# Decoder trunk with a state-space branch: buffers, load times and memory type of the state-space matrices and of the split u are changed

## The chip, the core and the metric

The kernel runs on one core of a Trainium2 chip. Its engines have instruction queues of their own and work beside each other: TensorE (PE, with PEld for the loading of its weights), VectorE (DVE), ScalarE (ACT), GpSimd (POOL) and SyncE (SP). The last two are used here mostly to issue transfers, which 16 DMA engines carry out. The metric is the device time of one execution in microseconds; less is better.

## The reference, cut to what matters

Two layers work on one sequence of 256 tokens of width 2048, all in float32. A layer has a mixer and an MLP:

```python
def hybrid_mixer(x, ...):
    q, k, v, u = parts of x @ w_in          # u: 1024 columns, 64 groups of 16
    gate_a, gate_s = sigmoid(x @ ...), sigmoid(x @ ...)
    attn = diff_attention(rope(q), rope(k), v, ...)
    ssm  = s5_ssm(u, ...)                   # a complex state of 64 per group
    merged = gate_a * (attn @ w_attn_up) + gate_s * (ssm @ w_ssm_up)
    return merged @ w_out

x = layer_norm(ALPHA * x + hybrid_mixer(x))
x = layer_norm(ALPHA * x + (relu(x @ w_mlp_up) ** 2) @ w_mlp_down)   # 2048 -> 8192 -> 2048

def s5_ssm(u, ...):                         # per group, per token
    bu = u @ b                              # 16 channels -> 64 complex states
    s  = running sum of bu with decay a     # the scan
    y  = Re(c s) + d u
    g  = gelu(y);  return g * sigmoid(g @ w_glu)
```

What matters below: `b` is made of four blocks per layer (here `bT`, 256 KB each, 1 MB per layer), u is the product of x with the first columns that a layer computes, and `bu` joins the two.

## The kernel before

**Products.** Every float32 product is done as three float32r products. An operand is split into a high part, which is the value rounded to float32r, and a low part, which is what is left: `split` copies the high part on ACT (L142) and subtracts it on DVE (L144). Then high x high, high x low and low x high are summed in PSUM. The weights pass through the core once: `load` fetches a chunk of 512 KB on SP's queue (L343) into one of four raw buffers (tile `w`), and splits it into `whi` and `wlo`, of which there are three each. One chunk is loaded ahead of the one in use (AHEAD = 1), and the scheduler puts the load as early as the buffers allow. A chunk feeds 24 matmuls of 256 columns in `gemm_feat` (L528 to L530), whose result has features on the partitions, or 12 of 512 columns in `gemm_tok` (L453, L454, L457).

**Background work.** The state-space branch, the attention and other small things are Python generators that `Background` runs beside the weight products: after each chunk `bg.pump(rate)` gives credit, and a generator runs until its `yield` costs have used it up. The rate is 2.0 a chunk in the mixer of layer 0, 1.8 in that of layer 1 and 0.3 in the MLP. So the order in which instructions are written comes from these costs; the scheduler then arranges each engine's queue. Each engine takes its queue in order.

**Buffers.** Scratch tiles of 128 x 512 come from two small sets: `t_bg` (tag `ss`, four buffers) for background work and `t_fg` (tag `at`, three) for evacuations of the products. Big tiles come from 17 slots of 8 KB per partition, and a slot is free again when the last reader of its tile is done.

**The state-space matrices.** `b_gen` handles the four blocks of a layer one after the other: it loads the block (L545, on POOL's queue) into an `ss` tile, splits it into two more (L142, L144), and writes high, low and high to a scratch tensor in DRAM, `bsplit` (L551, three writes of 256 KB). For layer 0 this runs in the first stage, behind the rotary tables and the parameters of the state space: `prep = [rope_gen(), ssm_param_gen(), b_gen(0)]`. For layer 1 it runs in the MLP of layer 0, as the first thing that is added to the background behind `down(0)`, ahead of tables (`emem`, `cmem`) for the same branch. There the load is held (`hold`) behind the products in front of it.

**u.** `u_evac` copies a finished part of u from PSUM to the slot `uT` (L891), splits it into two `at` tiles and writes three pieces to DRAM, `usplit` (L894, 256 KB each). A layer has four such parts, so 12 writes, in each layer's first products (layer 1: behind the first half of v).

**Where they meet.** `ssm_gen` loads, for each of 16 steps, a piece of `bsplit` (tile `bs`, L623) and a piece of `usplit` (tile `us`, L625) on POOL's queue, one buffer each, and multiplies them on PE (L646, four matmuls into `bu`). PE's queue holds these between the weight products.

Of the kernel before, what the change touches and what calls it, by code (L numbers as in the profile page):

```python
# [11 lines left out]
F32 = mybir.dt.float32  # L12
F32R = mybir.dt.float32r
# [7 lines left out]
P = 128  # L21
# [45 lines left out]


class Background:
    """Work that runs beside the weight products, a few instructions at a time."""  # L70

    def __init__(self):
        self.gens = []
# [31 lines left out]
def trunk(ctx: ExitStack, tc: tile.TileContext, A, out):  # L105
# [13 lines left out]
    def nm(s):  # L119
        uid[0] += 1  # L120
        return f"{s}_{uid[0]}"
# [4 lines left out]
    def t_bg(shape):  # L126
        return tmp.tile(shape, F32, tag="ss", name=nm("ss"), bufs=SS_BUFS)
# [20 lines left out]
    after = mybir.DependencyInfo(mybir.DependencyClass.NoSync, mybir.DependencyReason.DATA)  # L148

    class Chain:  # L150
        """Keeps instructions of one engine in the order given."""

        def __init__(self):
            self.last = None
# [268 lines left out]
    behind = mybir.DependencyInfo(mybir.DependencyClass.Sync, mybir.DependencyReason.DATA)  # L423

    def spread(dst, src):
        """Moves a [128, 2048] block in four parts, each behind the next products."""
        for c in range(4):
            cs = slice(c * W, c * W + W)
            drip.append((dst[:, cs], src[:, cs]))
# [1 line left out]
    recent = [None]  # L431

    def hold(i):
        """Keeps work that could run at any time behind the products in front of it."""
        if recent[0] is not None:
            tc.add_manual_dep(i.ins, recent[0].name, behind, reason="not before")
        return i
# [101 lines left out]
    bsplit, cmem, emem = {}, {}, {}  # L539

    def b_gen(l):
        bsplit[l] = dram.tile([4, 4, 3, 32, 2, 256], F32R, tag=f"bsplit{l}", name=f"bsplit{l}")
        for g in range(4):
            raw, hi, lo = (t_bg([P, 2, 256]) for _ in range(3))
            i = GP.dma_start(raw, A["bT"][l, g])  # L545
            if l > 0:
                hold(i)
            hi, lo = hi.bitcast(F32R), lo.bitcast(F32R)
            split(hi, lo, raw)
            for m, t in enumerate((hi, lo, hi)):  # L550
                GP.dma_start(bsplit[l][g, :, m], t)  # L551
            yield 0.6

    def e_steps(l, g, im, re, hold=lambda i: i):
# [49 lines left out]
    def ssm_gen(l, st):  # L604
# [13 lines left out]
        def operands(i):  # L618
            if i == 16:
                return None  # L620
            g, h, kk = i // 4, i // 2 % 2, i % 2
            bs = tmp.tile([96, 2, 2, P], F32R, tag="bs", name=nm("bs"), bufs=1)
            GP.dma_start(bs.rearrange("p q c s -> p q (c s)"), bsplit[l][g, 2 * kk:2 * kk + 2, :, :, h].rearrange("q m r s -> (m r) q s"))  # L623
            us = tmp.tile([96, 2, 256], F32, tag="us", name=nm("us"), bufs=1)
            GP.dma_start(us, st["split"][2 * kk:2 * kk + 2, :, :, 2 * g + h].rearrange("q m r t -> (m r) q t"))  # L625
            return bs, us
# [3 lines left out]
        for g in range(4):  # L630
# [10 lines left out]
            for k in range(4):  # L641
                bs, us = nxt
                bu = psa.tile([P, 2, 2, NCH, L], F32, tag="bu", name=nm("bu"), bufs=1)
                for q in range(2):
                    for ri in range(2):
                        PE.matmul(bu[:, q, ri].rearrange("p a b -> p (a b)"), bs[:, q, ri, :], us[:, q, :].bitcast(F32R), start=True, stop=True)  # L646
                nxt = operands(4 * g + k + 1)
                yield 0.3
                er = e_re[:, g, 2 * k:2 * k + 2, None, :].broadcast_to([P, 2, NCH, L])
                ei = e_im[:, g, 2 * k:2 * k + 2, None, :].broadcast_to([P, 2, NCH, L])  # L650
                wr, wi = (w[ri][:, :, 2 * k:2 * k + 2, :].rearrange("p c q t -> p q c t") for ri in range(2))
                ta, tb = t_bg([P, 2, NCH, L]), t_bg([P, 2, NCH, L])
                V.tensor_tensor(wr, bu[:, :, 0], er, op=ALU.mult)
                V.tensor_tensor(ta, bu[:, :, 1], ei, op=ALU.mult)
                V.tensor_tensor(wi, bu[:, :, 1], er, op=ALU.mult)
                yield 1.8
                V.tensor_tensor(tb, bu[:, :, 0], ei, op=ALU.mult)
                V.tensor_tensor(wr, wr, ta, op=ALU.add)
                V.tensor_tensor(wi, wi, tb, op=ALU.subtract)
                yield 1.8  # L660
# [205 lines left out]

        return evac

    prep = [rope_gen(), ssm_param_gen(), b_gen(0)]
    first = True  # L870

    for l in range(DEPTH):
# [9 lines left out]
        sgen = early()  # L882
        first = False
        uT = slot([P, 8, 256], name="uT")
        st["split"] = dram.tile([4, 3, 32, 8, 256], F32, tag=f"usplit{l}", name=f"usplit{l}")

        def u_evac(b, ps):
            ct = 4 * n + 2 * b
            u = uT[:, ct:ct + 2, :]
            hi, lo = t_fg([P, 2, 256]), t_fg([P, 2, 256])  # L890
            SC.activation(u, ps, AF.Copy)  # L891
            split(hi.bitcast(F32R), lo.bitcast(F32R), u)
            for m, t in enumerate((hi, hi, lo)):
                GP.dma_start(st["split"][:, m, :, ct:ct + 2], t)  # L894
# [192 lines left out]
def _layout(i):  # L1087
# [23 lines left out]
    for ri, s in enumerate(("re", "im")):  # L1111
        b = f["ssm_b_" + s].reshape(DEPTH, 8, 4, 2, 64, 16)
        c = f["ssm_c_" + s].reshape(DEPTH, 8, 4, 2, 16, 64)
        for g in range(2):
            bT[:, :, g, :, :, ri, g, :] = b[:, :, :, g].transpose(0, 2, 4, 1, 3)
            cT[:, g, :, ri, :, :, g, :] = c[:, :, :, g].transpose(0, 4, 1, 2, 3)
    o["bT"] = bT.reshape(DEPTH, P, 4, 2, 2 * P).transpose(0, 2, 1, 3, 4)
    o["cT"] = cT.reshape(DEPTH, P, 2, 4, 8, 32).transpose(0, 3, 1, 2, 4, 5)
    return {k: np.ascontiguousarray(v) for k, v in o.items()}

# [16 lines left out]
```

## Time and profile before

| | |
|---|---|
| runs, us | 2781.41, 2788.29, 2786.13 |
| median, us | 2786.13 |
| profiled execution, us | 2782.7 (its span; the page gives no time around the span) |
| PE busy | 2709.6 us, 97% |
| DVE busy | 1865.6 us, 67% |
| ACT busy | 1271.2 us, 46% |
| POOL busy | 146.4 us, 5% |
| DMA, mean over the span | 193 GB/s |

Shares of busy time are of the whole span. The slices of the span show where it is not alike. Each digit is a fortieth of the span, about 70 us, in tenths:

```profile
PE   7899999999999889999998999999999999999997
DMA  8756555674655666655748565556746565555673
```

The first slices, those at the 14th to 15th place (about 900 to 1040 us) and at the 22nd (about 1460 to 1530 us) are where PE is below nine tenths, apart from the last slice. In the first layer the u product starts the span; the 14th and 15th slice lie in the MLP of layer 0, and the 22nd in the u product of layer 1.

### The profile page before, as it was taken

The numbers are of one execution on the slowest core, as the hardware profiler recorded it, in microseconds if no ns is written. First come the engines' busy times: TensorE is split into PE (matmuls) and PEld (weight loads), VectorE is DVE, ScalarE is ACT, GpSimd is POOL, SyncE is SP. The second block draws the span as 40 slices with busy tenths as digits, with TensorE's granted clock in tenths as the row PEclk, the third lists the DMA queues.
The fourth block names the chain that finished last, engine by engine and source line by source line (L and its number), as shares of the span: only waits on it lengthen the run. The fifth ranks groups of instructions, "written<-read, shape, count | busy, mean of one in ns | idle before, by whom it ended". The sixth has DMA issues, their size and how long they took to land. (4 is left out here: it accounts for less than half of the span.)

```text
span 2782.7 us, 45210 instructions
## 1 busy us (share of the span) xinstructions
PE 2709.6 (97%) x18304; PEld 2487.0 (89%) x18304; DVE 1865.6 (67%) x2555; ACT 1271.2 (46%) x1635; POOL 146.4 (5%) x274
## 2 busy tenths in 40 slices
PE   7899999999999889999998999999999999999997
PEld 7889999988998888998788999999789989989876
DVE  5798999666655456655655998987766555545555
ACT  4554554544444344443443645544444444434442
POOL 2100000000000100000012000001000000000000
PEclk9999999999999999999999999999999999999999
DMA  8756555674655666655748565556746565555673
GB/s 269 202 182 198 173 168 167 212 238 131 207 182 189 186 196 205 222 189 194 237 154 238 176 191 175 168 174 222 255 131 203 183 194 186 188 191 184 193 230 127
DMA packets 169440, 536.27 MB, mean 193 GB/s; under 512 B 32112, under 2 KB 38288, under 8 KB 169232
## 3 DMA queue, kind: packets, MB, share of 16 engines
q1 hardware_dynamic: 133344, 482.40, 53.5%
q0 software_dynamic: 35888, 50.99, 6.9%
q8 instruction: 143, 2.34, 0.3%
q14 instruction: 65, 0.53, 0.1%
HBM read 513.32 MB, written 19.92 MB: 192 GB/s over the span
## 5 line engine op out<-in xcount | busy, mean ns | idle before, releaser
L144 DVE TENSOR_TENSOR wlo<-w,whi 128x1024 fp32r<-128x1024 f32 (+1 forms) x884 | 1076.8, 1220 | 696.1 <-ACT whi L142 694.6
L142 ACT ACTIVATE whi<-w 128x1024 fp32r<-128x1024 f32 (+1 forms) x884 | 934.0, 1058 | 1177.6 <-PE g L529 627.7
L528 PE MATMUL g<-xT,whi 128*128 128x256 f32 x3712 | 1058.0, 286 | 20.8 <-ACT whi L142 20.8
L530 PE MATMUL g<-xT,wlo 128*128 128x256 f32 x3712 | 1050.1, 287 | 23.3 <-DVE wlo L144 23.3
L529 PE MATMUL g<-xT,whi 128*128 128x256 f32 x3712 | 1056.9, 286 | 0.0
L528 PEld LDWEIGHTS g<-xT,whi 128*128 128x128 f32 x3712 | 722.0, 195 | 24.1 <-ACT whi L142 22.4
L530 PEld LDWEIGHTS g<-xT,wlo 128*128 128x128 f32 x3712 | 715.7, 195 | 28.6 <-DVE wlo L144 27.3
L529 PEld LDWEIGHTS g<-xT,whi 128*128 128x128 f32 x3712 | 721.9, 195 | 1.6 <-issue 1.2
L454 PE MATMUL g<-wlo,hT 128*128 128x512 f32 x972 | 379.1, 390 | 4.8 <-DVE wlo L144 4.8
L453 PE MATMUL g<-whi,hT 128*128 128x512 f32 x972 | 378.8, 390 | 0.8 <-ACT whi L142 0.8
L457 PE MATMUL g<-whi,hT 128*128 128x512 f32 x972 | 299.3, 389 | 0.0
L454 PEld LDWEIGHTS g<-wlo,hT 128*128 128x128 f32 x972 | 182.5, 188 | 44.9 <-DVE wlo L144 7.4
L453 PEld LDWEIGHTS g<-whi,hT 128*128 128x128 f32 x972 | 182.5, 188 | 40.1 <-ACT whi L142 2.8
L457 PEld LDWEIGHTS g<-whi,hT 128*128 128x128 f32 x972 | 182.5, 188 | 37.9
L454 PE MATMUL g<-wlo,merged 128*128 128x512 f32 x216 | 85.4, 395 | 2.6 <-DVE wlo L144 2.4
L453 PE MATMUL g<-whi,merged 128*128 128x512 f32 x216 | 84.3, 390 | 0.8 <-ACT whi L142 0.8
L671 DVE TENSOR_TENSOR_SCAN sw<-ss,sw 128x512 f32<-128x512 f32 x64 | 75.8, 1211 | 0.0
L529 PE MATMUL g<-sgl,whi 128*128 128x256 f32 x256 | 72.3, 283 | 0.0
L528 PE MATMUL g<-sgl,whi 128*128 128x256 f32 x256 | 72.0, 283 | 0.0
L530 PE MATMUL g<-sgl,wlo 128*128 128x256 f32 x256 | 72.0, 283 | 0.0
L529 PE MATMUL g<-ahl,whi 128*128 128x256 f32 x256 | 71.8, 284 | 0.0
L528 PE MATMUL g<-ahl,whi 128*128 128x256 f32 x256 | 71.4, 284 | 0.0
(284 smaller groups left out, 2774.3 us busy)
## 6 DMA issues: line engine op xcount, KB each, us to landing
w<-in_w_mlp_up_dram SPq DMA_DIRECT2D x256, 512.0 KB, 3.5
w<-in_w_mlp_down_dram SPq DMA_DIRECT2D x256, 512.0 KB, 3.6
w<-in_w_in_dram SPq DMA_DIRECT2D x255, 512.0 KB, 3.9
w<-in_w_out_dram SPq DMA_DIRECT2D x64, 512.0 KB, 4.4
w<-in_w_attn_up_dram SPq DMA_DIRECT2D x32, 512.0 KB, 3.7
w<-in_w_ssm_up_dram SPq DMA_DIRECT2D x32, 512.0 KB, 4.5
w<-in_w_glu_dram SPq DMA_DIRECT2D x16, 512.0 KB, 3.8
lnb<-in_ln_dram POOLq DMA_DIRECT2D x32, 256.0 KB, 4.6
```

Of the source, the lines that this page charges most:

```text
L142: SC.activation(hi, src, AF.Copy, scale=scale)
L144: V.tensor_tensor(lo, src, hi.bitcast(F32), op=ALU.subtract)
L453: mm(PE.matmul(ps[tt], act(kt)[:, 0, ts], hi[:, k, :], start=kt == 0, stop=False))
L454: mm(PE.matmul(ps[tt], act(kt)[:, 0, ts], lo[:, k, :], start=False, stop=False))
L457: mm(PE.matmul(ps[tt], act(kt)[:, 1, ts], hi[:, k, :], start=False, stop=kt == nkt - 1))
L528: m(PE.matmul(o, wh, ah, start=first and b % 2 == 0, stop=False))
L529: m(PE.matmul(o, wh, al, start=False, stop=False))
L530: m(PE.matmul(o, wl, ah, start=False, stop=last and b % 2 == 1))
L671: V.tensor_tensor_scan(wv, rg, wv, 0.0, ALU.mult, ALU.add)
```

## The change

`b_gen` gets buffers of its own from the slots: one for the four raw blocks (`braw`) and two for the split ones (`bhl`). The four loads are issued first, each held behind the products in front of it and 0.3 of credit apart. Then comes other work: in layer 0 the parameters of the state space, which stood ahead of `b_gen` before, and for layer 1 a pause of 2.0 of credit. Then the four blocks are split and written, 0.6 apart, and each high part is held behind the products in front of it. u's halves go to two slots (`uhl`) instead of `at` tiles. `bsplit` and the tile `bs` are plain float32, and the matmul reads `bs` as float32r. The host's layout of `bT` puts the four blocks of a partition side by side. The other edits empty comments.

```diff
     def b_gen(l):
-        bsplit[l] = dram.tile([4, 4, 3, 32, 2, 256], F32R, tag=f"bsplit{l}", name=f"bsplit{l}")
+        raw = slot([P, 4, 2, 256], name="braw")
         for g in range(4):
-            raw, hi, lo = (t_bg([P, 2, 256]) for _ in range(3))
-            i = GP.dma_start(raw, A["bT"][l, g])
-            if l > 0:
-                hold(i)
-            hi, lo = hi.bitcast(F32R), lo.bitcast(F32R)
-            split(hi, lo, raw)
+            hold(GP.dma_start(raw[:, g], A["bT"][l][:, g]))
+            yield 0.3
+        if l == 0:
+            yield from ssm_param_gen()
+        else:
+            yield 2.0
+        bsplit[l] = dram.tile([4, 4, 3, 32, 2, 256], F32, tag=f"bsplit{l}", name=f"bsplit{l}")
+        hi, lo = (slot([P, 4, 2, 256], name="bhl") for _ in range(2))
+        for g in range(4):
+            h = SC.activation(hi[:, g].bitcast(F32R), raw[:, g], AF.Copy)
+            hold(h)
+            V.tensor_tensor(lo[:, g].bitcast(F32R), raw[:, g], hi[:, g], op=ALU.subtract)
             for m, t in enumerate((hi, lo, hi)):
-                GP.dma_start(bsplit[l][g, :, m], t)
+                GP.dma_start(bsplit[l][g, :, m], t[:, g])
             yield 0.6
...
-            bs = tmp.tile([96, 2, 2, P], F32R, tag="bs", name=nm("bs"), bufs=1)
+            bs = tmp.tile([96, 2, 2, P], F32, tag="bs", name=nm("bs"), bufs=1)
...
-                        PE.matmul(bu[:, q, ri].rearrange("p a b -> p (a b)"), bs[:, q, ri, :], us[:, q, :].bitcast(F32R), start=True, stop=True)
+                        PE.matmul(bu[:, q, ri].rearrange("p a b -> p (a b)"), bs[:, q, ri, :].bitcast(F32R), us[:, q, :].bitcast(F32R), start=True, stop=True)
...
-    prep = [rope_gen(), ssm_param_gen(), b_gen(0)]
+    prep = [rope_gen(), b_gen(0)]
...
         uT = slot([P, 8, 256], name="uT")
+        uhl = [slot([P, 8, 256], name="uhl") for _ in range(2)]
...
-            hi, lo = t_fg([P, 2, 256]), t_fg([P, 2, 256])
+            hi, lo = (t[:, ct:ct + 2, :] for t in uhl)
...
-    o["bT"] = bT.reshape(DEPTH, P, 4, 2, 2 * P).transpose(0, 2, 1, 3, 4)
+    o["bT"] = bT.reshape(DEPTH, P, 4, 2, 2 * P)
```

The numbers of loads, splits, writes and matmuls are what they were. What moves is the order on ACT and POOL. On PE the weight products keep their order, and the first four `bu` matmuls of layer 0 stand behind 460 of them; before, one stood behind 412 and three behind 432.

ACT in the first stage, before, from its first state-space split on (`whi` is the high part of a weight chunk, `ss` of a state-space block, `uT` a part of u copied out of PSUM, `at` its high part):

```order
L142 ACTIVATE ss_501<-ss_500 128x512
L142 ACTIVATE whi_424<-w_422 128x1024
L142 ACTIVATE whi_471<-w_469 128x1024
L142 ACTIVATE ss_510<-ss_509 128x512
L142 ACTIVATE whi_547<-w_545 128x1024
L891 ACTIVATE uT_167<-g_170 128x512
L142 ACTIVATE whi_596<-w_594 128x1024
L142 ACTIVATE at_527<-uT_167 128x512
L891 ACTIVATE uT_167<-g_171 128x512
L287 ACTIVATE scr_315<-scr_315 128x64
L289 ACTIVATE scr_315<-scr_315 128x64
L142 ACTIVATE at_535<-uT_167 128x512
```

And after (`bhl` is the high part of a state-space block, `uhl` that of a part of u, L287 and L289 belong to the parameters):

```order
L142 ACTIVATE whi_530<-w_528 128x1024
L287 ACTIVATE scr_322<-scr_322 128x64
L289 ACTIVATE scr_322<-scr_322 128x64
L555 ACTIVATE bhl_507<-braw_317 128x512
L142 ACTIVATE whi_575<-w_573 128x1024
L900 ACTIVATE uT_167<-g_172 128x512
L900 ACTIVATE uT_167<-g_173 128x512
L142 ACTIVATE uhl_168<-uT_167 128x512
L555 ACTIVATE bhl_507<-braw_317 128x512
L142 ACTIVATE uhl_168<-uT_167 128x512
L555 ACTIVATE bhl_507<-braw_317 128x512 x2
L142 ACTIVATE whi_618<-w_616 128x1024
```

The first state-space split moves from behind the seventh weight split (`whi_377`) to behind the tenth (`whi_530`); the four now stand within two chunks, and all their loads are issued ahead of them.

POOL in the first stage, before, up to the first load of `us`; three writes of `bsplit` stand ahead of these rows (`ss` are blocks and their halves, `at` halves of u, `bs` and `us` the loads for `bu`):

```order
L551 DMA bsplit_499<-ss_510 4x32x512 x2
L545 DMA ss_518<-in_bT_dram 128x512
L623 DMA bs_896<-bsplit_499 96x2x256
L551 DMA bsplit_499<-ss_511 4x32x512
L894 DMA usplit_168<-at_527 4x32x512 x2
L894 DMA usplit_168<-at_535 4x32x512 x2
L894 DMA usplit_168<-at_528 4x32x512
L551 DMA bsplit_499<-ss_519 4x32x512 x2
L551 DMA bsplit_499<-ss_520 4x32x512
L545 DMA ss_575<-in_bT_dram 128x512
L894 DMA usplit_168<-at_536 4x32x512
L625 DMA us_898<-usplit_168 96x2x256
```

And after; two writes of `bsplit` stand ahead of these rows:

```order
L559 DMA bsplit_506<-bhl_508 4x32x512
L903 DMA usplit_170<-uhl_168 4x32x512 x2
L559 DMA bsplit_506<-bhl_507 4x32x512 x2
L903 DMA usplit_170<-uhl_168 4x32x512 x2
L903 DMA usplit_170<-uhl_169 4x32x512
L559 DMA bsplit_506<-bhl_507 4x32x512 x4
L559 DMA bsplit_506<-bhl_508 4x32x512
L903 DMA usplit_170<-uhl_169 4x32x512
L559 DMA bsplit_506<-bhl_508 4x32x512
L631 DMA bs_881<-bsplit_506 96x2x256
L559 DMA bsplit_506<-bhl_508 4x32x512
L633 DMA us_883<-usplit_170 96x2x256
```

No load of a block stands between the writes now, and 18 writes stand ahead of the first `us` where it was 15.

POOL in the MLP of layer 0, before, from the first block's load on:

```order
L545 DMA ss_9907<-in_bT_dram 128x512
L551 DMA bsplit_9906<-ss_9908 4x32x512 x2
L545 DMA ss_9976<-in_bT_dram 128x512
L551 DMA bsplit_9906<-ss_9909 4x32x512
L551 DMA bsplit_9906<-ss_9977 4x32x512 x2
L551 DMA bsplit_9906<-ss_9978 4x32x512
L545 DMA ss_10045<-in_bT_dram 128x512
L623 DMA bs_14694<-bsplit_9906 96x2x256
L551 DMA bsplit_9906<-ss_10046 4x32x512 x2
L545 DMA ss_10114<-in_bT_dram 128x512
L551 DMA bsplit_9906<-ss_10047 4x32x512
L551 DMA bsplit_9906<-ss_10115 4x32x512 x2
```

And after:

```order
L546 DMA braw_9891<-in_bT_dram 128x512 x4
L559 DMA bsplit_10211<-bhl_10212 4x32x512 x2
L559 DMA bsplit_10211<-bhl_10213 4x32x512
L559 DMA bsplit_10211<-bhl_10212 4x32x512 x2
L631 DMA bs_14664<-bsplit_10211 96x2x256
L559 DMA bsplit_10211<-bhl_10213 4x32x512
L559 DMA bsplit_10211<-bhl_10212 4x32x512 x2
L559 DMA bsplit_10211<-bhl_10213 4x32x512
L559 DMA bsplit_10211<-bhl_10212 4x32x512 x2
```

Each load stood behind a write of an earlier block, and the split needs the load; now the four loads stand ahead of all writes.

## Rows read from the trace of the kernel before

**Rows 1.** Page of the profile: span, and busy time of each engine.

```profile
span 2782.7 us, 45210 instructions
...
PE 2709.6 (97%) x18304; PEld 2487.0 (89%) x18304; DVE 1865.6 (67%) x2555; ACT 1271.2 (46%) x1635; POOL 146.4 (5%) x274
```

**Rows 2.** Stretches: us; busy of PE, PEld, DVE, ACT, POOL; clock; DMA share; GB/s.

```profile
25.00:100.00 75.00, 61.30 (x440) 59.88 (x441) 43.33 (x112) 27.89 (x37) 21.15 (x31) 0.89 0.84 237
720.00:740.00 20.00, 20.00 (x169) 20.00 (x168) 11.07 (x11) 9.48 (x12) 0.00 (x0) 1.00 0.57 189
940.00:1000.00 60.00, 44.75 (x284) 43.14 (x283) 22.34 (x25) 18.24 (x24) 10.07 (x16) 0.81 0.64 173
1455.00:1510.00 55.00, 46.85 (x365) 46.10 (x364) 26.54 (x31) 20.13 (x23) 16.79 (x26) 0.94 0.90 267
```

**Rows 3.** Waits of ACT, 25 to 100: waiting <- waited for, us, times, longest.

```profile
ACT ss L142 <- DMA ss<-in_bT_dram: 20.4, 3, 7.9
ACT whi L142 <- DMA w<-in_w_in_dram: 17.2, 5, 7.1
```

**Rows 4.** Waits, 900 to 1000 us.

```profile
ACT ss L142 <- DMA ss<-in_bT_dram: 28.4, 3, 13.1
...
DVE ss L560 <- DMA bsplit<-ss: 7.2, 1, 7.2
```

**Rows 5.** Timeline of ACT, MLP of layer 0: start, length; idle before in brackets.

```profile
968.17 0.63 ACT L142 ACTIVATE ss<-ss 128x512 fp32r<-128x512 f32 x1 [13.06 <-DMA ss<-in_bT_dram]
```

**Rows 6.** Timeline of POOL, same stretch.

```profile
952.56 2.03 POOL L551 DMA_DIRECT2D bsplit<-ss  x3 [11.71 <-ACT ss L142]
954.59 0.60 POOL L545 DMA_DIRECT2D ss<-in_bT_dram  x1
```

**Rows 7.** Waits, 1455 to 1510 us.

```profile
ACT whi L142 <- DMA w<-in_w_in_dram: 21.0, 5, 8.8
...
DVE at L144 <- DMA usplit<-at: 7.7, 1, 7.7
```

**Rows 8.** DMA issues, 935 to 1000: count, KB each, median us to landing.

```profile
w<-in_w_mlp_up_dram SPq DMA_DIRECT2D x14, 512.0 KB, 9.4
bsplit<-ss POOLq DMA_DIRECT2D x12, 256.0 KB, 10.1
ss<-in_bT_dram POOLq DMA_DIRECT2D x3, 256.0 KB, 12.0
emem<-ss POOLq DMA_DIRECT2D x2, 256.0 KB, 4.9
bs<-bsplit POOLq DMA_DIRECT2D x1, 192.0 KB, 14.1
```

**Rows 9.** Page: costliest groups; count, busy us, mean ns, idle before.

```profile
L144 DVE TENSOR_TENSOR wlo<-w,whi 128x1024 fp32r<-128x1024 f32 (+1 forms) x884 | 1076.8, 1220 | 696.1 <-ACT whi L142 694.6
```

**Rows 10.** Timeline of ACT, first stage.

```profile
30.99 1.06 ACT L142 ACTIVATE whi<-w 128x1024 fp32r<-128x1024 f32 x1 [1.44 <-PE g L529]
```

**Rows 11.** Timeline of POOL, first stage.

```profile
28.44 1.51 POOL L551 DMA_DIRECT2D bsplit<-ss  x2 [6.88 <-ACT ss L142]
...
65.66 0.67 POOL L625 DMA_DIRECT2D us<-usplit  x1 [6.52 <-DMA usplit<-at]
```

**Rows 12.** Timeline of PE, first stage.

```profile
75.52 0.28 PE L646 MATMUL bu<-us,bs 96*128 96x256 f32 x1
```

**Rows 13.** DMA issues, 25 to 100.

```profile
w<-in_w_in_dram SPq DMA_DIRECT2D x19, 512.0 KB, 9.6
bsplit<-ss POOLq DMA_DIRECT2D x12, 256.0 KB, 10.6
usplit<-at POOLq DMA_DIRECT2D x12, 256.0 KB, 15.0
...
us<-usplit POOLq DMA_DIRECT2D x2, 192.0 KB, 11.3
```

**Rows 14.** Page: DMA issues over the whole span.

```profile
w<-in_w_in_dram SPq DMA_DIRECT2D x255, 512.0 KB, 3.9
```

## The prediction

> **What bounds the kernel now.** The first view is the page: TensorE (PE) is busy 97% of the span [rows 1], so nothing off PE is worth anything unless PE waits for it there. The next question is where PE waits. The view by stretches shows three places. In a calm stretch PE does 169 matmuls in 20 us, 8.45 a microsecond, at a DMA share of 0.57 and 189 GB/s [rows 2]; that is the yardstick. In the first stage (25 to 100 us) it does 440 in 75 us. At its pace these need 52.1 us, so 22.9 us are lost. In the MLP of layer 0 (940 to 1000) it does 284 in 60 us: 33.6 us of work, 26.4 lost. In the u product of layer 1 (1455 to 1510) it does 365 in 55 us: 43.2 us of work, 11.8 lost. Part of the loss is idle time and part a lower granted clock behind it (0.89, 0.81 and 0.94 over these stretches, so partly at the lower of its two levels, 1.2 GHz, against 1.00 or 2.4 GHz in the calm one); counting matmuls takes both. Together 61.1 us, the most that this change can give back.
>
> The view of waits says why. PE waits for weight parts (`whi`, `wlo`), and their makers stand still. In the first stage ACT spends 20.4 us in three waits for the load of the state-space matrix, ahead of weight splits that could run [rows 3]. In the MLP of layer 0 it spends 28.4 us so, also in three waits, and DVE 7.2 us until a write of `bsplit` has landed, because the next scratch tile shares its buffers [rows 4]. ACT and DVE take their instructions in order, so one early split holds up every weight behind it. The chain of one of them: the load stands on POOL's queue behind three writes of the group before, it lands late, and ACT idles 13.06 us [rows 5, 6]. In layer 1 it is DVE, 7.7 us until a write of `usplit` frees an `at` tile [rows 7]. A second kind of wait stands beside these: ACT for the weights' own loads, 17.2 us in the first stage and 21.0 in layer 1 [rows 3, 7]. This kind the change does not touch.
>
> **The change part by part.** Splits and writes keep their count (4 ACT and 4 DVE splits, 12 writes per layer for the matrices; the same for u), so no engine gains work. The order of ACT and POOL tells what moves.
>
> *Layer 0's MLP.* The four loads are now issued a chunk or so apart, then 2.0 units of background credit pass, then come the splits 0.6 apart. At 0.3 credits a chunk these are (1.2 + 2.0 + 2.4) / 0.3 = 18.7 chunks of 24 matmuls, 2.84 us each by the yardstick: 53 us. The first split stands over 20 us behind its load, and a load took 12.0 us there in the median [rows 8]. So the 28.4 us of ACT waits go, and with own buffers the 7.2 us of DVE go. What is late next is the transfers: the stretch moved 0.64 x 60 = 38.4 us of all 16 DMA engines; its weights are 33.6 x 0.57 = 19.2 us of that, so the 18 other transfers listed there cost 19.2 us, about 1.07 us each [rows 2, 8]. Spread over 53 us they add 0.36 to 0.57: a share of 0.93, which fits, barely. The splits' hold behind a product costs ACT nothing while it comes with the release of a weight buffer that ACT awaits anyway; if that cover is gone it is 1.06 + 1.22 us a split [rows 9, 10], below 10 in all. Between 15 and 26 us returned; I take 24, near the full loss, since the share fits.
>
> *First stage.* All four loads go out in one piece and their splits come behind the first chunks, after the parameters. The 20.4 us of ACT waits go. But here the DMA engines are nearly full: 0.84 x 75 = 63 us of work [rows 2]. The same bytes cannot take less than 63 us (12 us returned), and at the 0.90 that the stretch in layer 1 sustained they take 70 (5 returned). The second half of the u writes may land later, where the share is low: six writes at 1.07 us, up to 6 more. On the other side POOL's queue now has 18 writes ahead of the first load of `us`, and before 15. Before, those from 28.44 on and the loads between took until 65.66 us: 37.2 us for 15 writes, 2.5 us a write [rows 11]. The first split now stands behind ACT's tenth weight split; the ninth started at 30.99 [rows 10], and a chunk later the writes can begin, at about 36 us. At the old pace the load would then be issued at 81 and, with the 11.3 us that such a load took [rows 13], land at 92.3. PE's first `bu` product, with all weight products queued behind it, stands behind 460 weight products in the new order and behind 412 in the old, where it started at 75.52 [rows 12]. At this stretch's 5.87 products a microsecond the 48 more are 8.2 us, so it would be due at 83.7, and the stage would be 9 us slower. But much of that 2.5 us was POOL waiting for ACT's late splits, and this goes. Between -9 and 18 returned; I take 11, nearer the share's bound than the old pace.
>
> *u product of layer 1.* Own tiles for both halves end DVE's 7.7 us. The transfers need 0.90 x 55 = 49.5 us [rows 2], so by them 5.5 us can go at most if all stay in the stretch, and all 11.8 if the last writes slip out of it. ACT's 21.0 us of waits for weights [rows 7] are the transfers' own and stay. Between 0 and 11; I take 5, the share's bound.
>
> *Plain float32 memory.* The matmul reads the same bits. No row prices the type alone: a write of `bsplit` took 10.6 us to land and one of the plainly typed `usplit` 15.0 in the same stretch [rows 13], so the trace sees no cost; the bound is zero below and, if a write became half as dear, 12 x 0.5 = 6 us of DMA time in the first stage. I take zero. The Trainium skill, "DMA: Bandwidth & Descriptors", section "SWDGE vs HWDGE vs iDMA", says that a float32r source is read as float32, so that a float32r destination always casts; by it the old writes were casts and the new ones are not. That row of landings does not show a cast to be slower; by the page alone the sum would stay, or gain those 6 us.
>
> **Sum.** 24 + 11 + 5 = 40 us. The profiled span is 2782.7 us; the page gives no time around it, and the runs shown have a median of 2786.1 (2781.4 to 2788.3), 3.4 above the span. A saving counts alike in both: 2786 - 40 = 2746 us. The ends of the terms give 6 to 55 saved: 2731 to 2780.
>
> A second reckoning from other rows: weights live in four raw buffers, so a landing time L feeds a chunk per (L + 1.06 + 1.22) / 4 us, and PE wants one per 2.84. The stretch factor is (L + 2.3) / 11.4. With the medians of today, 9.4 to 9.6 us [rows 8, 13], it is 1.03 to 1.04, and nearly the whole 61 us would return. With 11 us it is 1.17; the 128.9 us of work in the three stretches would take 150 of today's 190, again 40 saved.
>
> **Rivals.** *The transfers keep most of it.* With the splits out of the way POOL queues writes in longer runs, and weights and writes contend. For it: weights land in 9.4 to 9.6 us instead of 3.9 wherever writes are queued [rows 8, 13, 14]. If weights had half of the 237 / 0.84 = 282 GB/s of the first stage, 141 of the 189 they need, PE would run at 0.75: the first stage takes 69.5 us (5.5 saved), layer 1's 57.6 (2.6 lost), and in the MLP 19.2 us of other transfers at half the engines last 38 us and cost 9.6 (17 saved). Sum 20: 2766 us. Beside it stands a rule: the same page of the Trainium skill, section "Queues, rings and completion order", says that each DMA engine takes turns between its queues packet by packet, and that leaves neither queue in front. The rows of today, PE at a full clock in the calm parts between, agree with neither side alone. Against it: in the MLP the loads and splits are spaced.
>
> *Slower than before: the weights starve for good.* The place is the four raw buffers, the price the factor above. Breakeven is 128.9 x f = 190, f = 1.47, L = 14.5 us; each further microsecond costs 11.3. A `usplit` write already takes 15.0 [rows 13]; at 16 us for the weights all three stretches together take 207, 17 slower: 2803. Against it: no weight median today is above 9.6.
>
> *It does not do what it says.* Three more tiles of the 17 slots per layer for the matrices and two for u: in the MLP 4 xT, 2 x, 8 hT and these 3 are just 17. If a slot is released late (its write must land first), an `hT` evacuation on ACT waits as the split did. Then some 26 us return to the stretch and the rest is within noise: about 2783. Against it: the writes are over tens of microseconds before the last `hT` tile.
>
> *More than I take:* the writes get cheaper without the cast and late ones slip out: 55 to 60 saved, 2728.
>
> **How the numbers follow.** Forecast (2731 to 2764): 0.70. Transfers keep most (2764 to 2775): 0.13. More (under 2731): 0.08. Late slots, no change: 0.05. Starved weights: 0.04. 0.3% is 8.4 us, about what can be told from no change. Faster by more than that: 0.70 + 0.08 + nearly all of 0.13 = 0.90; within: 0.06; slower: 0.04. The range leaves out the starved case, most of the slot case and the edges of the others: 2727 to 2770.
>
> **What will show it.** In the first stage and in the MLP no ACT wait for `braw`, and the MLP stretch at 8.4 matmuls a microsecond with a clock of 1.00; that term is the surest. In the first stage a DMA share above 0.9, weight waits for the DMA instead of for splits, and the first `bu` between 68 and 88 us. No DVE wait for `usplit` in layer 1, but PE still waiting for `us` there. I am wrong if ACT waits for `braw` or a slot, if weights land in over 13 us for long, or if PE stands at the first `bu` beyond 92 us.

## The result and the profile after

The changed kernel takes 2758.84 us (median of four runs, 2752.28 to 2763.52) against 2787.05 us before (2781.41 to 2788.29): a ratio of 0.9899, 95% interval 0.9884 to 0.9914. That is 28 us saved where 40 were forecast. The profiled execution has a span of 2754.7 us, 28.0 below that of before. The heads of the page, to be read beside [rows 1]:

```profile
span 2754.7 us, 45201 instructions
...
PE 2696.3 (98%) x18304; PEld 2477.0 (90%) x18304; DVE 1865.6 (68%) x2555; ACT 1272.5 (46%) x1635; POOL 145.7 (5%) x274
```

Where the 28 us came from is read from two instructions that stand at the same place of the program in both kernels: POOL's load of the first block for layer 1, which is held behind the products that end `down(0)`, and POOL's first write of `usplit` in layer 1. The timeline of POOL, before (start, length, instruction):

```profile
933.05 0.54 POOL L545 DMA_DIRECT2D ss<-in_bT_dram  x1 [227.64 <-PE g L530]
...
1457.88 1.45 POOL L894 DMA_DIRECT2D usplit<-at  x2 [1.67 <-ACT at L142]
```

And after:

```profile
933.00 0.54 POOL L546 DMA_DIRECT2D braw<-in_bT_dram  x1 [227.89 <-issue]
...
1436.78 1.44 POOL L903 DMA_DIRECT2D usplit<-uhl  x2 [1.67 <-ACT uhl L142]
```

The load starts at 933.00 where it was 933.05: the first stage returned nothing. (The load stands far behind that stage. Counted by weight products in the traces, product 700, at about 120 us, starts 2.2 us later than before; in the kernels below the two counts differ by up to 3 us.) From the load to the write 21.1 us are gone (524.83 to 503.78), all of it in the MLP. From the write to the end of the span another 6.9 (1324.82 to 1317.92). So the terms of the sum, 24 + 11 + 5, came out in this execution as 21.1 + 0.0 + 6.9.

The stretches after, for the first three of [rows 2]; the fourth is the u product of layer 1, here 70 us from about 5 us ahead of its first write:

```profile
25.00:100.00 75.00, 60.61 (x434) 59.30 (x435) 49.58 (x123) 31.21 (x43) 19.31 (x29) 0.86 0.87 240
720.00:740.00 20.00, 20.00 (x169) 20.00 (x169) 11.08 (x11) 9.48 (x12) 0.00 (x0) 1.00 0.59 184
940.00:1000.00 60.00, 57.10 (x458) 56.28 (x456) 33.28 (x37) 25.84 (x31) 9.50 (x14) 0.97 0.77 223
1432.00:1502.00 70.00, 65.58 (x542) 65.03 (x542) 44.79 (x54) 32.38 (x38) 20.02 (x33) 1.00 0.83 264
```

and the same 70 us of the kernel before:

```profile
1453.00:1523.00 70.00, 61.85 (x489) 61.10 (x488) 37.28 (x45) 30.03 (x36) 18.38 (x29) 0.95 0.82 241
```

The MLP went from 284 to 458 matmuls in 60 us and from a clock of 0.81 to 0.97. Layer 1's u product went from 489 to 542 in 70 us and from 0.95 to 1.00. The first stage does 434 matmuls where it did 440.

The waits of the first stage, after (who waits, for what, us, times, longest):

```profile
ACT whi L142 <- DMA w<-in_w_in_dram: 27.4, 7, 9.2
...
POOL usplit L903 <- DMA bsplit<-bhl: 12.9, 3, 9.5
...
POOL us L633 <- DMA bsplit<-bhl: 6.7, 1, 6.7
...
PE bu L654 <- DMA us<-usplit: 4.2, 1, 4.2
```

Beside [rows 3]: the 20.4 us for `ss` are gone, no ACT instruction waits for `braw`, and the wait for the weights' own loads grew from 17.2 to 27.4 us. The DMA issues of the same stretch, beside [rows 13]:

```profile
w<-in_w_in_dram SPq DMA_DIRECT2D x19, 512.0 KB, 11.5
bsplit<-bhl POOLq DMA_DIRECT2D x12, 256.0 KB, 17.2
usplit<-uhl POOLq DMA_DIRECT2D x12, 256.0 KB, 16.1
```

A weight chunk lands 11.5 us after its issue (9.6 before, both medians), a write of `bsplit` 17.2 (10.6). Counted from issues and landings in the traces, eight of POOL's transfers were on their way at once for 16.8 of these 75 us before and for 36.6 now. ACT stood twice for 9 us while eight writes were on their way:

```profile
56.92 1.06 ACT L142 ACTIVATE whi<-w 128x1024 fp32r<-128x1024 f32 x1 [9.24 <-DMA w<-in_w_in_dram]
66.89 1.06 ACT L142 ACTIVATE whi<-w 128x1024 fp32r<-128x1024 f32 x1 [8.91 <-DMA w<-in_w_in_dram]
```

In the MLP both waits of [rows 4] are gone, and two others are there:

```profile
ACT whi L142 <- DMA w<-in_w_mlp_up_dram: 9.0, 3, 5.0
POOL bs L631 <- DMA bsplit<-bhl: 8.3, 1, 8.3
```

### The profile page after: what moved, and what is told of

Its sections match the earlier page's. It is cut to its first block, busy times and chain, and to the rows that moved or that the text cites. A ratio compares the mean times of both kernels' runs of the same rounds, so it can differ in the third digit from the quotient of the medians.

```text
span 2754.7 us, 45201 instructions
## 1 busy us (share of the span) xinstructions
PE 2696.3 (98%) x18304; PEld 2477.0 (90%) x18304; DVE 1865.6 (68%) x2555; ACT 1272.5 (46%) x1635; POOL 145.7 (5%) x274
## 5 line engine op out<-in xcount | busy, mean ns | idle before, releaser
L528 PE MATMUL g<-xT,whi 128*128 128x256 f32 x3712 | 1053.3, 285 | 17.2 <-ACT whi L142 17.2
```

Of the source, the lines that this page charges most:

```text
L528: m(PE.matmul(o, wh, ah, start=first and b % 2 == 0, stop=False))
```

## The experiments

One table first. For each kernel it holds the times of the two marks, the span of its profiled execution, and the us returned against the kernel before: up to the first mark (first stage), between the marks (MLP of layer 0), behind the second (u product of layer 1 and what follows). The four kernels below `before` have the same order on every engine in the first stage (e1 with another memory type), so their differences there are spread. Each row is a single profiled execution: in e1, e4, e5, e8 and e11 it is the quickest of that kernel's runs (in e4 by 9 us), in e2, e6, e7 and e10 the slowest.

| kernel | writes a layer | first mark | second mark | span | first stage | MLP | rest |
|---|---|---|---|---|---|---|---|
| before | 24 | 933.05 | 1457.88 | 2782.7 | | | |
| changed | 24 | 933.00 | 1436.78 | 2754.7 | 0.0 | 21.1 | 6.9 |
| e10, changed again | 24 | 933.99 | 1433.19 | 2757.7 | -0.9 | 25.6 | 0.3 |
| e8, bs load held | 24 | 924.60 | 1425.03 | 2747.3 | 8.4 | 24.4 | 2.5 |
| e1, float32r memory | 24 | 926.98 | 1431.39 | 2749.2 | 6.1 | 20.4 | 7.0 |
| e6, wider spacing | 24 | 932.68 | 1434.47 | 2756.1 | 0.4 | 23.0 | 3.2 |
| e7, later bu | 24 | 927.59 | 1434.45 | 2757.2 | 5.5 | 18.0 | 2.1 |
| e2, matrices only | 24 | 935.17 | 1437.93 | 2762.5 | -2.1 | 22.1 | 0.2 |
| e3, u only | 24 | 934.82 | 1460.14 | 2781.8 | -1.8 | -0.5 | 3.2 |
| e5, 3 of 12 matrix writes | 15 in layer 0 | 921.82 | 1422.02 | 2742.1 | 11.2 | 24.6 | 4.7 |
| e4, high parts once | 16 | 916.01 | 1419.48 | 2736.5 | 17.0 | 21.4 | 7.8 |
| e9, once and bs held | 16 | 921.07 | 1419.88 | 2741.8 | 12.0 | 26.0 | 2.9 |
| e11, and wider spacing | 16 | 916.08 | 1415.67 | 2733.8 | 17.0 | 25.2 | 6.7 |
| e12, and later bu | 16 | 917.98 | 1416.91 | 2740.6 | 15.1 | 25.9 | 1.1 |

**The type alone (e1).**

```diff
-        bsplit[l] = dram.tile([4, 4, 3, 32, 2, 256], F32, ...)
+        bsplit[l] = dram.tile([4, 4, 3, 32, 2, 256], F32R, ...)
...
-            bs = tmp.tile([96, 2, 2, P], F32, ...)
+            bs = tmp.tile([96, 2, 2, P], F32R, ...)
```

> The changed kernel with bsplit and bs put back to float32r, nothing else. Theory A (as predicted: the type costs nothing): no stretch moves, 2759 us within its own spread of some 6 us. Rival B (a write with the cast occupies the DMA engines longer, as the packet count of POOL's queue, 35888 before and 25136 after, would allow): the MLP of layer 0 gives back more than the 6 us of now behind its peak and the first stage loses 5 to 10 us: 2766 to 2775 us.

2752.71 us, ratio to before 0.9885 (0.9859 to 0.9911), which is the changed kernel's ratio within its interval. The row of POOL's DMA queue (packets, MB, share of the 16 engines) with float32r memory, and after it that of the changed kernel:

```profile
q0 software_dynamic: 35888, 50.99, 6.9%
```

```profile
q0 software_dynamic: 25136, 50.99, 6.6%
```

Plain memory saves 10,752 packets and 0.3% of the engines' span, and no time that can be seen. Theory A holds as far as an interval of 7 us to either side can tell; nothing shows that the packets of the cast crowded the weights.

**Each part alone (e2, e3).**

```diff
-        uhl = [slot([P, 8, 256], name="uhl") for _ in range(2)]
...
-            hi, lo = (t[:, ct:ct + 2, :] for t in uhl)      # e2: the changed kernel without the slots for u
+            hi, lo = t_fg([P, 2, 256]), t_fg([P, 2, 256])
```

```diff
+        uhl = [slot([P, 8, 256], name="uhl") for _ in range(2)]
...
-            hi, lo = t_fg([P, 2, 256]), t_fg([P, 2, 256])   # e3: the kernel before with them
+            hi, lo = (t[:, ct:ct + 2, :] for t in uhl)
```

> The changed kernel with u's halves back in the three at tiles; the state-space matrices as changed. If the parts are separate: the MLP of layer 0 keeps its 21 us, layer 1 loses its 7 us, the first stage stays where it was: 2766 us. Rival: in the first stage the at tiles meter the u writes, so they leave gaps for weights; then the first stage is up to 6 us faster than with both parts and the time about 2760 us.

> The kernel before with u's halves in slots of their own; matrices as before. If the parts are separate: layer 1 returns 7 us, MLP and first stage as before: 2780 us. Rival (slots for u hold up other tiles, or u's writes come in longer runs and hit the late b loads of the first stage): 2787 us or more.

e2: 2762.9 us, 0.9911 (0.9886 to 0.9936). e3: 2784.76 us, 1.0000 (0.9985 to 1.0015). So the matrices' buffers and early loads carry nearly all of the gain, and the slots for u alone carry none that can be measured. In e2 the MLP kept its gain (22.1) and layer 1 lost it (0.2), as expected of separate parts; its rival, a first stage up to 6 us faster, was not seen (-2.1). In e3 layer 1 was to return 7 us and 3.2 are there, so this expectation was missed. In e3's u product of layer 1 the waits are these:

```profile
ACT whi L142 <- DMA w<-in_w_in_dram: 12.9, 3, 7.6
...
PE bu L646 <- DMA us<-usplit: 6.7, 1, 6.7
```

DVE's 7.7 us for an `at` tile [rows 7] are gone as meant, ACT's waits for weights fell from 21.0 to 12.9, and PE's wait at `bu` for `us` rose from 3.0 to 6.7. In the kernel before it was this:

```profile
PE bu L646 <- DMA us<-usplit: 3.0, 1, 3.0
```

The freed writes go out sooner and in one run, but `us` lies on the same queue behind them, and PE comes to it sooner.

**Fewer writes (e4, e5).** e4 writes each high part once and loads it twice:

```diff
-            for m, t in enumerate((hi, lo, hi)):
+            for m, t in enumerate((hi, lo)):
...
-            GP.dma_start(bs..., bsplit[l][g, 2 * kk:2 * kk + 2, :, :, h]...)
+            GP.dma_start(bv[:64], bsplit[l][g, 2 * kk:2 * kk + 2, :, :, h]...)
+            GP.dma_start(bv[64:], bsplit[l][g, 2 * kk:2 * kk + 2, 0, :, h]...)
...
+            GP.dma_start(us[32:], st["split"][2 * kk:2 * kk + 2, :, :, 2 * g + h]...)
+            GP.dma_start(us[:32], st["split"][2 * kk:2 * kk + 2, 0, :, 2 * g + h]...)
...
-            for m, t in enumerate((hi, hi, lo)):
+            for m, t in enumerate((hi, lo)):
```

> The changed kernel with each high part written once: 8 writes a layer for the matrices and 8 for u where there are 12 and 12; bs and us are loaded in two parts each, the high part twice. Theory T (the first stage is bound by transfers): 8 writes less at 1.07 us give 8 to 9 us in the first stage, 3 to 5 in the MLP of layer 0 and up to 3 in layer 1: 2743 to 2748 us. Rival P (POOL's queue and its issues bound it; each bs and us takes one more issue): the first stage gains nothing, 2755 us or more.

e5 keeps the form and leaves out nine of layer 0's writes:

```diff
-            for m, t in enumerate((hi, lo, hi)):
+            for m, t in enumerate((hi, lo, hi) if l or g == 0 else ()):
...
-bsplit[l][g, 2 * kk:2 * kk + 2, :, :, h]
+bsplit[l][g if l else 0, 2 * kk:2 * kk + 2, :, :, h]
```

> The changed kernel, but in layer 0 only the first of the four blocks is written to bsplit (3 writes in place of 12; its later steps read that block, so layer 0's states are not the reference's). Theory T (the first stage is bound by transfers): 9 writes less at 1.07 us return about 10 us in the first stage, so weight product 700 comes 8 to 14 us earlier than in the changed kernel. Rival P (the place of the first us load on POOL's queue, with PE waiting at the first bu, sets it): also faster, since fewer writes stand ahead; told apart from T by the next run. Rival S (the loss is in the order of ACT and DVE, which is the same here): no gain.

e4: 2747.63 us, 0.9852 (0.9827 to 0.9878), clear of the changed kernel's interval. e5: 2748.45 us, 0.9869 (0.9836 to 0.9902), which overlaps it. The first stage (25 to 100 us) of e4 and of e5, to be read beside the changed kernel's row above:

```profile
25.00:100.00 75.00, 71.77 (x578) 71.04 (x579) 65.83 (x149) 43.60 (x59) 18.36 (x29) 0.98 0.84 256
```

```profile
25.00:100.00 75.00, 69.31 (x539) 68.91 (x540) 60.70 (x142) 42.03 (x59) 13.89 (x22) 0.93 0.79 238
```

578 and 539 matmuls where the changed kernel did 434, and the weights landed sooner there:

```profile
w<-in_w_in_dram SPq DMA_DIRECT2D x24, 512.0 KB, 6.4
```

```profile
w<-in_w_in_dram SPq DMA_DIRECT2D x23, 512.0 KB, 6.1
```

The first stage returned 17.0 and 11.2 us, against 0.0, -0.9, 8.4 and 6.1 of the changed order with its 24 writes (mean 3.4). In e5 product 700 comes 13.1 us earlier than in the changed kernel, inside the 8 to 14 of theory T. Rival P of e4, no gain in the first stage, and rival S of e5 fail. The profiled execution of e4 was its quickest; e9 below, with the same order in that stage, returned 12.0. The 3 to 5 us that T gave e4 in the MLP are not there (21.4 returned, where the changed kernel's two executions have 21.1 and 25.6).

**Is it the place of `us` in the queue? (e7)** Fewer writes also shorten POOL's queue ahead of `us`. e7 leaves the queue as it is and lets PE meet `bu` later:

```diff
-        st["u"] = uT
+        if l > 0:
+            st["u"] = uT
...
                 gemm_feat(weights("w_in", l, base + n), act, NKT, rope_evac(dst, n, scale))
+                st["u"] = uT
```

> The changed kernel, but in layer 0 the state-space steps are allowed to begin one product later, so that the first bu stands behind 556 weight products on PE's queue where it was 460; all writes stay as they are. Theory T (transfers): the writes still crowd the weights out, product 460 comes no earlier than in the changed kernel (within 4 us). Rival P (PE waits for us at bu): PE runs on past the old place, product 500 comes 5 us or more earlier.

2755.91 us, 0.9896 (0.9865 to 0.9926). The first stage returned 5.5 us, inside the spread of the changed order (-0.9 to 8.4). What PE still waited for between 60 and 160 us:

```profile
PE g L530 <- DVE wlo L144: 4.2, 7, 1.0
PE g L528 <- ACT whi L142: 3.7, 3, 1.8
PE bu L654 <- DMA us<-usplit: 0.6, 1, 0.6
```

The wait at `bu` shrank from the 4.2 us of the changed kernel to 0.6, and waits for weights of 7.9 us stay. Counting weight products in the traces, product 500 starts 9.1 us earlier than in the kernel before. By the letter that is P's mark (the profiled changed kernel has it 1.4 us later than before), but e8, with `bu` in its old place, has it 6.1 earlier, and by product 700 e7 is 4.2 ahead of before and e8 5.4. So PE's wait at `bu` is real, and taking it away left nothing beyond the spread. With fewer writes it is the same: e12 below, with `bu` behind 624 products, returned 15.1 us in the first stage, and e11, with `bu` behind 480, 17.0. But a few us cannot be told from nothing in this way. In e10 below, the changed kernel again, PE waited longer there than in its first execution:

```profile
ACT whi L142 <- DMA w<-in_w_in_dram: 28.0, 7, 11.6
...
PE bu L654 <- DMA us<-usplit: 9.3, 1, 9.3
```

In that execution product 460, the last ahead of `bu`, came 5.0 us earlier than before, and product 500 came 3.0 later: what the first stage had gained went at `bu`. The `us` load stands behind the same writes on POOL's queue, so both of PE's waits, for weights and for `us`, come from these transfers; how much of the loss goes through which stays open.

**The `bs` load among the writes (e8), and spacing (e6).**

```diff
-            GP.dma_start(bs.rearrange("p q c s -> p q (c s)"), ...)
+            (hold if l > 0 and i == 0 else free)(GP.dma_start(bs.rearrange("p q c s -> p q (c s)"), ...))   # e8
```

```diff
-            yield 0.6                       # e6, behind the writes of a block
+            yield 1.2 if l else 2.0
```

> The changed kernel with the first bs load of layer 1 held back, so that it leaves the middle of the bsplit writes in the MLP of layer 0, where POOL waits 8.3 us in front of it and then issues seven writes in one run. Theory H (this wait bunches the writes, and the bunch makes weights late): of the 5.6 us that the MLP gives back behind its peak 3 to 5 come back, 2754 us. Rival T2 (the writes cost that in any spacing this close): the give-back stays at 5 to 6 us, 2759 us.

> The changed kernel with its splits further apart: 2.0 of credit in the first stage (one chunk) and 1.2 in the MLP of layer 0 (four chunks, some 11 us), where both were 0.6. Theory T: in the first stage all 24 writes still fall into the same 60 us, so no more than 4 us beyond the changed kernel's own spread; in the MLP, where there is room, the 5.6 us given back shrink to 2 or less, even with the bs load in its place: 2754 us. Rival (spacing alone is the answer in both): the first stage returns 10 us more, 2745 us.

e8: 2755.03 us, 0.9889 (0.9868 to 0.9910). e6: 2756.13 us, 0.9875 (0.9850 to 0.9900). Both intervals overlap the changed kernel's. POOL in the MLP of the changed kernel:

```profile
962.21 2.12 POOL L559 DMA_DIRECT2D bsplit<-bhl  x3 [20.29 <-ACT bhl L555]
967.97 1.37 POOL L559 DMA_DIRECT2D bsplit<-bhl  x2 [3.64 <-ACT bhl L555]
977.68 0.66 POOL L631 DMA_DIRECT2D bs<-bsplit  x1 [8.34 <-DMA bsplit<-bhl]
978.33 2.76 POOL L559 DMA_DIRECT2D bsplit<-bhl  x4
982.80 1.37 POOL L559 DMA_DIRECT2D bsplit<-bhl  x2 [1.70 <-ACT bhl L555]
986.04 0.69 POOL L559 DMA_DIRECT2D bsplit<-bhl  x1 [1.88 <-DVE wlo L144]
```

and with the load held:

```profile
953.81 2.13 POOL L559 DMA_DIRECT2D bsplit<-bhl  x3 [20.29 <-ACT bhl L555]
959.57 2.05 POOL L559 DMA_DIRECT2D bsplit<-bhl  x3 [3.63 <-ACT bhl L555]
965.33 2.05 POOL L559 DMA_DIRECT2D bsplit<-bhl  x3 [3.71 <-ACT bhl L555]
971.79 1.37 POOL L559 DMA_DIRECT2D bsplit<-bhl  x2 [4.41 <-ACT bhl L555]
973.33 0.69 POOL L559 DMA_DIRECT2D bsplit<-bhl  x1 [0.17 <-issue]
```

The wait of 8.34 us in front of `bs` and the run of seven writes behind it are gone, and the writes go out three at a time. In the table the four kernels with the load held (e8, e9, e11, e12) return 24.4 to 26.0 us in the MLP, close to the whole loss of 26.4. Those with the load in place and the changed matrices return 18.0 to 25.6, two of them (e10, e5) as much as the former. So the wait is seen and the direction fits theory H, but the executions with the load in place spread too widely to call it settled. The held load goes out among the writes of u in layer 1 instead, at 1453.01 us, and PE waits for it there:

```profile
PE bu L654 <- DMA bs<-bsplit: 6.8, 1, 6.8
```

So e8 gave back behind the second mark (2.5 returned, against 6.9 in the changed kernel and 0.3 in e10) some of what the MLP gained. In e6, with the load in place, POOL stood 13.3 us there and the MLP returned 23.0, 3.4 short of the whole loss where 2 or less was expected; its first stage returned 0.4. That speaks for theory T and against spacing as the answer where all 24 writes must still go through the same 60 us, by one profiled execution; of e6's other runs one took 2743.76 us.

**The changed kernel again (e10).**

> The changed kernel once more, unchanged, for the spread of its stretches between executions. Two kernels with the same order in the first stage as this one put weight product 700 between 2 us later and 5 us earlier than the kernel before, so the first stage returns 0 to 5 us by the transfers' view, and the MLP 20 to 22. If the first stage is fixed at a return of zero by something in the order, product 700 comes 2 us late again.

2758.17 us, 0.9896 (0.9881 to 0.9911). The first stage came out at -0.9, so about zero again, the MLP at 25.6, above the 20 to 22 expected, and the u product of layer 1 at 0.3. Product 700 was 3.8 us late, which is the mark that was named for a return held at zero by the order; the 8.4 and 6.1 us of e8 and e1 under the same order speak against that, though they are other programs. Weights landed sooner than in the first execution, and sooner than before (9.6), at the same ACT wait for them (28.0 us, shown above):

```profile
w<-in_w_in_dram SPq DMA_DIRECT2D x19, 512.0 KB, 8.9
```

So the median of 11.5 us is not a steady trait of the changed kernel; the long waits are, and so is the time with eight transfers on their way (37.2 us of 75). In the u product of layer 1 PE waited longer at `bu` than in the first execution (4.4 us in three waits):

```profile
PE bu L654 <- DMA us<-usplit: 8.1, 2, 4.2
```

So the two later terms trade a few us between executions of one program; their sum was 28.0 and 25.9.

**Putting it together (e9, e11, e12).** e9 is e4 with both first `bs` loads of layer 1 held as in e8; e11 adds e6's spacing; e12 adds e7's edit for both layers.

> Both together: each high part written once and the first bs load of layer 1 held back. First stage as with the high parts written once (15 us returned), and of the 5 us that the MLP still gives back there with POOL waiting 10.3 us at bs, 3 to 5 returned: 2743 us, the fastest so far. If the spacing does not matter: 2748 us.

> High parts written once, first bs load of layer 1 held back, and the wider spacing of both stages. If spacing adds nothing to fewer writes: 2744 us as without it. If it adds in the first stage where the 16 writes leave gaps to fill: 2738 to 2741 us.

> High parts written once, bs load held back, wider spacing, and in both layers the state-space steps may begin one product later, so that PE meets the first bu some 100 weight products later. If PE's wait at bu for us is what is left in the u product of layer 1 (8.1 us of it in one execution of the changed kernel, 4.4 in another): layer 1 returns 10 to 11 us of its 11.8 and the time is 2735 to 2737 us. If weights that land late are what is left: 2739 us as without it. If the later state-space branch is then waited for before the GLU: slower than 2739 us.

e9: 2743.93 us, 0.9847 (0.9823 to 0.9872). e11: 2739.09 us, 0.9831 (0.9814 to 0.9848): the lowest median, 48 us below before. All three are clear of the changed kernel's interval. e9's time is the 2743 expected; e11's lies in the range given for spacing that adds in the first stage, but its interval overlaps that of e9, so what spacing adds is not settled. e12: 2743.49 us, 0.9854 (0.9827 to 0.9881), not faster. The u product of layer 1 (70 us from the same place) of e11 and of e12:

```profile
1411.00:1481.00 70.00, 68.05 (x553) 67.61 (x552) 45.01 (x54) 33.19 (x39) 22.51 (x40) 0.98 0.81 255
```

```profile
1412.00:1482.00 70.00, 70.00 (x586) 70.00 (x585) 41.20 (x45) 34.49 (x40) 17.85 (x30) 1.00 0.85 262
```

With `bu` later PE does not stand in that stretch at all (70.00 us busy, 586 matmuls against 553). But behind it, from 1750 to 1850 us, it is late:

```profile
1750.00:1850.00 100.00, 99.31 (x842) 97.67 (x841) 82.11 (x126) 47.87 (x67) 0.00 (x0) 1.00 0.56 171
```

```profile
1750.00:1850.00 100.00, 96.06 (x795) 91.39 (x790) 87.68 (x139) 44.40 (x67) 6.88 (x13) 1.00 0.54 165
```

842 matmuls against 795, with DVE busier (82.11 against 87.68 us). Counted by weight products, e12 gains 4.5 us on e11 from the second mark to product 9,200 and loses 10.1 between products 10,500 and 12,000: the third expectation, that the later state-space branch is paid for behind. Which wait takes it there was not followed.

## Why the prediction came out as it did

**What bounds the kernel.** Right. The three stretches held 61.1 us by the counting of matmuls, and e11 returned 48.9 us with edits to the splits, buffers and transfers of the matrices and of u alone.

**Layer 0's MLP: 24 us forecast, 21.1 measured and 25.6 in the second execution.** Right in mechanism and size. The waits for blocks and for scratch are gone, and transfers are late next, as said. The signs named for it, 8.4 matmuls a microsecond and a clock of 1.00, were not quite reached (458 in 60 us are 7.6, at 0.97). What the working left out is the first `bs` load of layer 1 between the writes: it needs a write that has not landed, so POOL stands and the writes bunch. It stood among them in the kernel before too, and was there to be read in the order of POOL. That it costs the missing few us is argued, not shown (e8).

**First stage: 11 us forecast; 0.0 and -0.9 measured in two executions, 8.4 and 6.1 in e8 and e1 with the same order.** This is the step that failed. It said that "at the 0.90 that the stretch in layer 1 sustained they take 70 (5 returned)", plus up to 6 for late writes. The share was 0.87 (0.81 in e10; above 0.9 was named as a sign), but a share says how busy the DMA engines are and not for whom. With the splits no longer late, eight transfers were on their way for 36.6 us of the stretch instead of 16.8 (37.2 in e10), and ACT's waits for blocks (20.4 us) turned into more waits for weights (17.2 to 27.4, and 28.0 in e10) and a wait of PE at the first `bu` (4.2 and 9.3 us, none before). That fewer writes bring 11.2 to 17.0 us back (e4, e5, e9, e11, e12) shows that the writes are the cause. The second reckoning of the prediction does not carry it: by its factor (L + 2.3) / 11.4, 11.5 us make 1.21, while 434 matmuls in 75 us at the yardstick's pace make 1.46; in e10 8.9 us make less than 1, and its 421 matmuls 1.51. A median landing time misses the few long waits and the wait at `bu`. Product 700, the end of what the burst reaches, lay 2.2 and 3.8 us later than before.

A sub-step failed in the same way. The pace of the writes was to improve on the old 2.5 us, since "much of that 2.5 us was POOL waiting for ACT's late splits, and this goes". From 38.31 to 80.19 us POOL issued 18 writes, 2.3 us each, and `us` went out at 80.19 where 81 was worked out for the old pace: POOL now waited for landings instead, 12.9 us at `usplit` for writes of `bsplit` and 6.7 at `us`. In the trace POOL's transfers use eight semaphores in turn, and a ninth is issued only when the first has landed: the write at 53.84 us followed a landing at 53.6. This held in the kernel before as well. The first `bu` started at 89.1 (90.3 in e10), just past the 68 to 88 that were named. The bound of 9 us lost at that place was near for the wait (4.2 and 9.3 us); the stage as a whole came out at zero because product 460, just ahead of it, came 1.0 and 5.0 us earlier than before.

**Layer 1: 5 us forecast, 6.9 and 0.3 measured in two executions.** Around the forecast in the mean, and the mechanism half right. DVE's wait went, and PE went on waiting for `us`, as said; that this wait would grow (3.0 to 4.4 and 8.1 us) was not. In single executions a term of this size cannot be told from the spread.

**Plain float32: nothing forecast, nothing found (e1).** The Trainium skill's page "DMA: Bandwidth & Descriptors" calls a float32r destination a cast always (section "SWDGE vs HWDGE vs iDMA"); the fewer packets agree with a difference of that kind, and the possible price of 6 us was not seen, with intervals of 4 and 7 us to either side.

**The rivals.** "The transfers keep most of it" is what happened in the first stage and there alone: 5.5 us were named for it, and of the four executions two lie below that and two above (mean 3.4). For the whole it named 2766 us; the measured 2758.84 lies between this and the forecast of 2746. The rule that stood beside it (the Trainium skill, "DMA: Bandwidth & Descriptors", section "Queues, rings and completion order": the engines take turns between queues) agrees with the first stage, in that weights issued while six or more of POOL's transfers were on their way took 13.4 us on average in the changed kernel and 12.7 in e10, and those issued beside three or fewer 6.8 and 4.2. No run separates it from other ways of sharing. The weights did not starve for good (medians of 11.5 and 8.9 us against the breakeven of 14.5), and no instruction waited for a slot in the places looked at.

**The sum.** 40 us were forecast and 28 came. The missing 12 are the 11 of the first stage and 2.9 of the MLP, less 1.9 that layer 1 gave more. The total stayed inside the range of 2727 to 2770 us because the MLP, the largest term, came out near its forecast and the range was wide enough for a first stage of zero; that says nothing for the first stage's working.

## What to carry to other kernels

Where a wait for late data is removed in a stretch whose DMA engines are already over 0.8 busy, ask first who else is waiting for these engines there: here the time came back as waits for weights and for `us`. Taking bytes away from that stretch was worth more than moving or buffering them: eight of 24 writes less returned some 11 us there (14.5, the mean of e4 and e9, against 3.4), about 1.4 us a write where 1.07 had been reckoned. With single executions on both sides the difference from 1.07 is not shown; by the ratios of all runs the 16 writes less of e4 are worth 13 us in the whole kernel, 0.8 us each. And a load placed among writes, which needs one of them, turned spaced transfers into a burst; holding it back moved its wait to the place where it was needed.

## What had not been expected of the hardware

Where the DMA engines are fullest, the first stage returned -0.9, 0.0, 6.1 and 8.4 us under one order of instructions. The first two are two executions of one program and the others are programs that differ elsewhere, so how much of this is chance from execution to execution is not shown; whole runs of the changed kernel lie between 2752.28 and 2763.52 us. A stage's gain below some 9 us can't be read there from a single profile.
